# Halving the PSUM pools at the seams of a two-layer diffusion backbone, and modulation vectors first in the work paced beside attention

## The chip, the cores and the metric

The kernel runs on one core of a Trainium2 chip. The metric is the device time of one execution in microseconds; given is the median of three runs.

## What is computed

Two transformer layers over 512 latent tokens with 256 context tokens ahead of or beside them, width 1024, float32. Layer 0 mixes tokens by windowed grouped-query attention (16 heads of 64, 4 key heads, a sink logit, a window of 128 latent neighbours plus all context keys), layer 1 by a bidirectional gated linear recurrence (HGRN2). Each layer ends in a gated channel mixer with a 3-tap convolution. Every part is normalised and modulated first:

```python
def layer(x, ctx, mixer):
    h = rms_norm(x) * (1 + scale) + shift      # shift, scale, gate = SiLU(c) @ ada_w
    x = x + gate * mixer(h)                    # attention, or HGRN2
    h = rms_norm(x) * (1 + scale2) + shift2
    u, g = split(h @ w_up)                     # 2816 wide each
    x = x + gate2 * ((conv3(u) -> silu) * g) @ w_down
    return x
...
s = concat([q @ k_window, q @ k_ctx, sink])    # one softmax, sink column dropped
```

Latent and context rows are modulated by vectors of their own. The output is the latent stream.

## The kernel before, in words

Products are float32 split into a high and a low part (wh, wl for weights), so each needs three matmuls. A tile framework schedules the program: the order in which the program is written gives each instruction its priority, a simulated timeline orders each engine's queue, and tiles come from pools. PSUM has eight banks of 512 float32 columns. A pool opened where an older pool was closed lies over the same banks, and its first tile waits for the last users of those banks. So which pool lies where sets what a stage's first matmul waits for. Weights come in raw through two buffers of 1 MB (`wp`, tile `wr`; the modulation weights `wada` use the same two), SyncE issues the loads in program order, ACT copies a high part (L117, L140) and DVE makes the low part (L118, L141).

The stages, with their places in the profiled execution:

- First norm and the key and value projections, to about 97 us. Its last pools are psP0 (banks 0 to 2), psP1 (3 to 5) and psTA (6 and 7).
- Attention, 97 to 358 us (`attention`). 4 key groups times 6 query tiles are 24 units. `attend` computes scores S for four heads of a unit (L785, L786), their maximum nm on DVE (L809), exponentials on ACT (L795), and normalises on POOL (L797); query tiles of the context have tiles Sc and Pc. `weigh`, one unit later, transposes the weights of the softmax (pt, L829), copies them out (L832, L834) and multiplies with V (pv, L837, copied out as o in L839). `q_proj` projects a query group (pjq, L611). PSUM: psS 2 buffers of 2 banks (0 to 3), psT (4, 5), psV (6), psP (7).
- Beside attention runs paced work, the generator `others` (L851 to L860): after each unit, steps are taken until they have cost `PER_UNIT`. Its items are the query projections of groups 1 to 3 and two sets of modulation vectors (`ada_steps`, L301: eight k-steps, each one load of 1 MB and four matmuls `ada`, and a last step that transposes the result, `adat`).
- Output projection, 342 to 424 us (`attn_out`, product ao, transposes xT of the input x; `add_gated` evicts on DVE, L908). ao's pool pj lies in banks 0 to 3, that of xT, ppA, in 4 to 7.
- First channel mixer, 424 to 977 us: up products in sums and differences of halves (tiles pZ, pY, pV, L188, from part sums hs that DVE makes, L384), statistics nss and nR, down products dn (L170) evicted by DVE (L1024, tiles xl, xc). All tiles come from one pool of eight banks in turn.
- HGRN, 977 to about 1425 us (its first product is pf, from the normalised hn), with the pools sc (0, 1), pj (2 to 5) and lv (6, 7); its output product ho, to 1453.
- Second channel mixer, 1454 to 1821 us, for latent rows alone, again from one pool of eight banks; row factors from the sum of squares acc (nss, L536).

Of the kernel before, what the change touches and what calls it, by code (L numbers as in the profile page):

```python
# [14 lines left out]
PSUM = bass.MemoryType.PSUM  # L15
# [57 lines left out]
class Kernel:  # L73
    def __init__(self, tc, a, dbg=None):
        self.tc, self.nc, self.a, self.dbg = tc, tc.nc, a, dbg or {}
# [576 lines left out]
    def attention(self, hn):  # L652
        nc, a, tc = self.nc, self.a, self.tc
        win = a["attn_w_in"][0]
        es = ExitStack()
# [90 lines left out]
        with e1:  # L746
            tmp = self.ap_ = self.pool(e1, "atmpA", 2)
            self.ap_tag = "qraw"
            psP = kv["pool"]
            psT = self.pool(e1, "psTA", 2, PSUM)  # L750
# [7 lines left out]
        qp.append(self.pool(es, "qp1", 1))  # L758
        pb = self.pool(es, "pb", 3)
        sm = self.pool(es, "sm", 3)  # L760
        psS = self.pool(es, "psS", 2, PSUM)
        psT = self.pool(es, "psT", 2, PSUM)
        psV = self.pool(es, "psV", 1, PSUM)
        psP = self.pool(es, "psP", 1, PSUM)
        ORD = (0, 2, 1, 3)

        def attend(g, qt):
# [26 lines left out]
            def finish(j, sp, p, n):  # L794
                nc.scalar.activation(p[:, :n + 1], sp, AF.Exp, bias=nm[:, j:j + 1], accum_out=den[:, j:j + 1])  # L795
                nc.vector.reciprocal(r[:, j:j + 1], den[:, j:j + 1])
                nc.gpsimd.tensor_scalar(p[:, :n], p[:, :n], r[:, j:j + 1], 1.0, op0=ALU.mult, op1=ALU.mult)  # L797
                pr.append(p)

            if lat:  # L800
                masks = ([(lo, 128)] if qt > 0 else []) + ([(LAT - P, 256)] if qt < NQ - 1 else [])
                for j, h in enumerate(ORD):
                    if j % 2 == 0:
                        p = pb.tile([P, 2, 644], F32, tag="P", name="P", bufs=4)
                    sp = psS.tile([P, 1024], F32, tag="S", name="S")
                    scores(sp, lo, h, kb0 * P, (kb1 + 1) * P, masks)
                    scores(sp, LAT, h, LAT, TOK, [])
                    sink_col(sp, TOK, h)
                    nc.vector.tensor_reduce(nm[:, j:j + 1], sp[:, lo:TOK + 1], axis=AX.X, op=ALU.max, negate=True)  # L809
                    finish(j, sp[:, lo:TOK + 1], p[:, j % 2], nk)  # L810
            else:
                for j0 in (0, 2):
                    p = pb.tile([P, 2, 644], F32, tag="P", name="Pc", bufs=4)
                    sp = psS.tile([P, 2, 512], F32, tag="S", name="Sc")
                    for j in range(2):
                        scores(sp[:, j], 0, ORD[j0 + j], LAT, TOK, [])
                        sink_col(sp[:, j], CTX, ORD[j0 + j])
                    nc.vector.tensor_reduce(nm[:, j0:j0 + 2], sp[:, :, :CTX + 1], axis=AX.X, op=ALU.max, negate=True)
                    for j in range(2):
                        finish(j0 + j, sp[:, j, :CTX + 1], p[:, j], CTX)  # L820
# [30 lines left out]
        def others():  # L851
            def ada(l, r):
                for _ in self.ada_steps(l, r, psP, "pj", 512):
                    yield 0.9

            yield from q_proj(psP, psT, 1)
            yield from ada(0, 1)
            for g in (2, 3):
                yield from q_proj(psP, psT, g)
            yield from ada(0, 2)  # L860

        work = others()
# [92 lines left out]
    def ffn(self, l, hs, R, rows, lat_only, tmp, acp, bk, gp, done, side=None):  # L955
        nc, a = self.nc, self.a
# [41 lines left out]
        for r, nf in enumerate(ROUNDS[l]):  # L998


            coming = list(range(f0 + nf, f0 + nf + (*ROUNDS[l], 0)[r + 1]))
            ahead = []
            for dp in range(KT // 2):
                if len(ahead) < len(coming) and (lat_only or dp == 0):
                    ahead.append(up(coming[len(ahead)]))
                if side and r < 5 and dp == 0:
                    next(side, None)
                w = self.load_w([wdn[f0 * P:(f0 + nf) * P, dp * 256:dp * 256 + 256].rearrange("(k p) m -> p k m", p=P)], True)
                outs = [[(bank("dn")[:, 0:m], c) for _, c, m in segs] for _ in range(2)]

                def down(j, ks):
# [308 lines left out]
    def run(self, stop=99):  # L1320
        nc, a = self.nc, self.a
# [17 lines left out]
        self.wsp.append(wsC)  # L1339
        Rp = self.pool(top, "Rp", 1)  # L1340
        pjs = ExitStack()
        pj = self.pool(pjs, "pj", 2, PSUM)
        hB = ExitStack()
        hb = self.pool(hB, "hB")
        h1 = hb.tile([P, 4, 2, 4, 386], F32R, tag="hn", name="hs0")
# [3 lines left out]
        es = ExitStack()  # L1349
# [3 lines left out]
        hs = [*(h1[:, i] for i in range(4)), h2]  # L1353
        with ExitStack() as e2:
            pp = self.pool(e2, "ppA", 2, PSUM)
            xsp = self.pool(e2, "xsp", 2)
            self.attn_out(oh, hs, acc, _Multi(tmp, xsp, ("xs",)), pj, pp)
        pjs.close()
        rs.close()
        if stop == 2:  # L1360
            self.dump_x(); es.close(); hss.close(); hB.close(); top.close(); return
        bk = self.pool(pjs, "bkA", 8, PSUM)
        h3 = self.pool(rs, "hs2", right=True).tile([P, 2, 2, 4, 386], F32R, tag="hs", name="hs5")
        hs += [h3[:, i] for i in range(2)]
        gp = self.pool(es, "gpA", 5)
# [24 lines left out]
        es = ExitStack()  # L1390
# [2 lines left out]
        self.wsp = [self.ws0, wsC, self.ws0, wsD]  # L1393
        e2 = ExitStack()
        sc = self.pool(e2, "sc", 2, PSUM)
        pj = self.pool(e2, "pj", 2, PSUM)
        lv = self.pool(e2, "lv", 2, PSUM)
        part = self.hgrn(hn2[0], R, accs[0], hb, pj, lv, sc)
        hc = self.pool(rs, "hC", 1, right=True)
        hs1 = hc.tile([P, 7, 2, 4, 258], F32R, tag="hs", name="hs3")  # L1400
# [15 lines left out]
        gp = self.pool(es, "gpB", 9)  # L1416
        self.wsp = [self.ws0, wsC, self.ws0, wsD, self.pool(es, "wsE", 2)]
        self.wd = self.pool(es, "wd", 2)
        bk = self.pool(es, "bkB", 8, PSUM)
        rows = self.row_factor(acc, True, tmp, bk, "ps", 512, R, -1.0, (gp, "g"))  # L1420
        ost = {}

# [21 lines left out]
class _Halves:  # L1444
# [5 lines left out]
    def tile(self, *a, **kw):  # L1450
        return self.parts.pop(0)


class _Multi:


# [28 lines left out]
```

## Time and profile before

| | |
|---|---|
| median of 3 runs | 1826.52 us (1824.79 to 1827.17) |
| profiled execution | 1823.13 us, its span 1821.1 us |
| mean granted TensorE clock | 0.995 of full |
| TensorE matmul busy | 97% of the span |
| TensorE weight loads | 85% |
| DVE, ACT, POOL | 73%, 46%, 14% |
| HBM read | 162 MB, 90 GB/s |

Every instruction runs on its engine's queue in order. A timeline row gives start, busy time, engine, line, operation, output from inputs, and, in brackets, how long the engine stood idle before it and what released it. Rows of the same kind are joined with their count. The columns of the table of stretches are the length, busy time and instructions of TensorE's matmuls, its weight loads, DVE, ACT and POOL, then the granted clock, the share of DMA time and the rate.

### The profile page before, as it was taken

What the parts mean: (1) busy time and instruction counts of PE and PEld (TensorE: products, weight loads), DVE (VectorE), ACT (ScalarE), POOL (GpSimd) and SP (SyncE); (2) the same over time, 40 slices, a digit from 0 to 9 for tenths busy, and PEclk for the clock granted to TensorE, in tenths of its full rate; (3) what the DMA queues carried; (4) which work ended last, traced back from release to release, by engine and by line L of the source; (5) the groups of instructions that cost most, each with busy time, mean ns of one, the idle gap of its engine ahead of it and who ended that gap; (6) DMA issues with size and microseconds to landing.
All of it is one profiled execution on the core that took longest, in us unless ns stands there. A gap on an engine that the chain in (4) does not pass through costs nothing.

```text
span 1821.1 us, 32329 instructions
## 1 busy us (share of the span) xinstructions
PE 1762.3 (97%) x13062; PEld 1542.3 (85%) x13062; DVE 1327.0 (73%) x2420; ACT 840.9 (46%) x1754; POOL 253.2 (14%) x233
## 2 busy tenths in 40 slices
PE   6999999998999999999999999999999989999998
PEld 4986786687889888999998888889886789999997
DVE  6575576467777775867877667777776789998985
ACT  4344555465534452534455333333332556555553
POOL 1233233200101010101100101111110012011110
PEclk9999999999999999999999999999999989999999
DMA  9203203332333343221214221111225234333222
GB/s 310 76 24 140 70 24 139 85 106 88 110 110 107 114 139 93 93 70 58 71 44 122 59 59 39 56 48 47 59 71 185 71 93 118 107 112 105 84 69 81
DMA packets 204611, 166.44 MB, mean 91 GB/s; under 512 B 5341, under 2 KB 198446, under 8 KB 199342
## 3 DMA queue, kind: packets, MB, share of 16 engines
q1 hardware_dynamic: 196800, 160.47, 28.8%
q10 hardware_dynamic: 7662, 3.92, 0.7%
q8 instruction: 102, 1.67, 0.4%
q14 instruction: 47, 0.39, 0.1%
HBM read 162.27 MB, written 2.10 MB: 90 GB/s over the span
## 4 chain that ended last, share of the span: by engine, by line
PE 87%; DVE 5%; DMA 4%; ACT 2%; issue 1%; SPq 0%; POOL 0%; ACTq 0%; DVEq 0%; POOLq 0%
PE dn L170 16%; PE pZ L188 15%; PE pf L170 8%; PE pV L188 7%; PE pjq L611 4%; PE pv L170 4%; PE pY L188 4%; PE ao L170 4%; PE pgate L170 3%; PE pq L170 3%; PE pv L837 3%; PE pt L829 2%; PE ho L170 2%; PE kv L611 2%; PE ada L309 2%; DMA wr<-in_ffn_w_up 2%
## 5 line engine op out<-in xcount | busy, mean ns | idle before, releaser
L188 PE MATMUL pZ<-hs,wh 128*128 128x386 f32 (+1 forms) x1408 | 315.9, 314 | 4.7 <-DVE xl L908 1.5
L140 ACT ACTIVATE wh<-wr 128x512 fp32r<-128x512 f32 x264 | 163.3, 629 | 236.2 <-PE pZ L188 85.5
L170 PE MATMUL dn<-g,wh 128*128 128x512 f32 (+1 forms) x1056 | 266.0, 357 | 0.1
L188 PEld LDWEIGHTS pZ<-hs,wh 128*128 128x128 f32 x1408 | 240.9, 191 | 18.4 <-issue 7.8
L117 ACT ACTIVATE wh<-wr 128x512 fp32r<-128x512 f32 (+2 forms) x192 | 113.4, 601 | 280.8 <-PE pf L170 75.7
L141 DVE TENSOR_TENSOR wl<-wr,wh 128x512 fp32r<-128x512 f32 x264 | 190.8, 732 | 47.3 <-ACT wh L140 42.9
L188 PE MATMUL pZ<-hs,wl 128*128 128x386 f32 (+1 forms) x704 | 218.1, 313 | 3.2 <-DVE wl L141 3.2
L170 PEld LDWEIGHTS dn<-g,wh 128*128 128x128 f32 x1056 | 172.8, 188 | 26.1 <-ACT wh L117 0.4
L923 POOL TENSOR_TENSOR gg<-gg,R 128x772 f32<-128x772 f32 (+1 forms) x44 | 92.5, 2101 | 727.1 <-DVE gg L922 637.9
L118 DVE TENSOR_TENSOR wl<-wr,wh 128x512 fp32r<-128x512 f32 (+2 forms) x192 | 132.2, 698 | 70.3 <-ACT wh L117 58.2
L188 PE MATMUL pV<-hs,wh 128*128 128x386 f32 (+1 forms) x704 | 160.7, 314 | 2.4 <-DVE hs L384 1.8
L170 PE MATMUL dn<-g,wl 128*128 128x512 f32 (+1 forms) x528 | 158.9, 356 | 0.0
L188 PEld LDWEIGHTS pZ<-hs,wl 128*128 128x128 f32 x704 | 133.3, 190 | 6.7 <-DVE wl L141 4.8
L188 PEld LDWEIGHTS pV<-hs,wh 128*128 128x128 f32 x704 | 120.9, 191 | 5.2 <-DVE hs L384 2.8
L170 PE MATMUL pf<-hn,wh 128*128 128x512 f32 (+1 forms) x512 | 117.6, 344 | 2.5 <-DVE xc L1024 1.9
L188 PE MATMUL pV<-hs,wl 128*128 128x386 f32 (+1 forms) x352 | 110.5, 314 | 0.3 <-DVE wl L141 0.3
L170 PEld LDWEIGHTS dn<-g,wl 128*128 128x128 f32 x528 | 87.5, 188 | 14.2
L1024 DVE SCALAR_TENSOR_TENSOR xl<-dn,mod,xl 128x512 f32<-128x512 f32 x96 | 71.3, 747 | 37.2 <-PE dn L170 37.0
L170 PEld LDWEIGHTS pf<-hn,wh 128*128 128x128 f32 x512 | 79.2, 189 | 15.0 <-DVE xc L1024 2.2
L188 PE MATMUL pY<-hs,wh 128*128 128x386 f32 (+1 forms) x352 | 80.3, 313 | 4.6 <-ACT wh L140 4.3
L611 PE MATMUL pjq<-wh,hn 128*128 128x256 f32 x384 | 77.8, 290 | 0.0
L188 PEld LDWEIGHTS pY<-hs,wh 128*128 128x128 f32 x352 | 59.3, 189 | 10.5 <-ACT wh L140 8.7
(301 smaller groups left out, 3853.4 us busy)
## 6 DMA issues: line engine op xcount, KB each, us to landing
wr<-in_ffn_w_up SPq DMA_DIRECT2D x88, 512.0 KB, 5.0
wada<-in_ada_w SPq DMA_DIRECT2D x40, 1024.0 KB, 4.8
wr<-in_hgrn_w_in SPq DMA_DIRECT2D x40, 512.0 KB, 4.0
wd<-in_ffn_w_down SPq DMA_DIRECT2D x20, 512.0 KB, 4.0
ar<-in_ada_w SPq DMA_DIRECT2D x32, 256.0 KB, 7.0
wr<-in_attn_w_in SPq DMA_DIRECT2D x6, 1024.0 KB, 8.4
wr<-in_ffn_w_down SPq DMA_DIRECT2D x12, 384.0 KB, 3.2
wr<-in_attn_w_out SPq DMA_DIRECT2D x8, 512.0 KB, 5.1
```

The source lines that it names most:

```text
L117: nc.scalar.activation(wh, src, AF.Copy)
L118: nc.vector.tensor_tensor(wl, src, f(wh), op=ALU.subtract)
L140: nc.scalar.activation(ops[i][0], src, AF.Copy)
L141: nc.vector.tensor_tensor(ops[i][1], src, f(ops[i][0]), op=ALU.subtract)
L170: nc.tensor.matmul(o, lhsT=wt, rhs=at[:, t0:t0 + o.shape[1]], start=(first and n == 0 and i == 0), stop=(last and n == len(ks) - 1 and i = ...
L188: self.nc.tensor.matmul(ps, lhsT=wt, rhs=at, start=(first and k == 0 and i == 0), stop=(k == nk - 1 and i == 2), skip_group_check=not first)
L309: nc.tensor.matmul(ps[32 * j:32 * j + 32, 0:512], lhsT=self.cs[:, k, :], rhs=raw[:, j * 512:(j + 1) * 512], start=(k == 0), stop=(k == KT ...
L611: nc.tensor.matmul(out, lhsT=x, rhs=y[:, wk], start=(start and k == 0 and j == 0), stop=(stop and k == KT - 1 and j == 2))
L829: nc.tensor.transpose(pt[:, j * P:(j + 1) * P], pr[j][:, b * P:(b + 1) * P], self.ident)
L837: nc.tensor.matmul(pv[a * HD:(a + 1) * HD, 0:256], lhsT=V[:, tl, g, :], rhs=pT[:, a * 256:(a + 1) * 256], start=(b == 0), stop=(b == len(t ...
L923: times = lambda eng, o, x, y: eng.tensor_tensor(o, x, y, op=ALU.mult)
L1024: nc.vector.scalar_tensor_tensor(x[:, d], o, self.modc(l, v, 5, d), x[:, d], op0=ALU.mult, op1=ALU.add)
```

## The change

Every stage's PSUM pools are cut into smaller ones or change places, so that tiles lie over other banks. `_Turn` hands out tiles from its pools by turns, after those in `first`. In attention S tiles alternate between psS0 (banks 0, 1) and psS1 (3, 4), pt between psT0 (2) and psT1 (6), with psP in 5 and psV in 7. In the output projection ppA now lies in banks 0 to 3 and pj in 4 to 7. Both channel mixers have two pools of four banks; in the last round of the first, the last two steps take all their four banks from one of them each. In HGRN lv changes places with pj. The paced work starts with the first set of modulation vectors, and three of its steps are taken unpaid inside the very first unit, after head j=1. No instruction is added or removed.

```diff
-        psS = self.pool(es, "psS", 2, PSUM)
-        psT = self.pool(es, "psT", 2, PSUM)
+        psS0 = self.pool(es, "psS0", 1, PSUM)
+        psT0 = self.pool(es, "psT0", 1, PSUM)
+        psS = _Turn([psS0, self.pool(es, "psS1", 1, PSUM)])
+        psP = self.pool(es, "psP", 1, PSUM)
+        psT = _Turn([psT0, self.pool(es, "psT1", 1, PSUM)])
         psV = self.pool(es, "psV", 1, PSUM)
-        psP = self.pool(es, "psP", 1, PSUM)
...
                     finish(j, sp[:, lo:TOK + 1], p[:, j % 2], nk)
+                    if g == 0 and qt == 0 and j == 1:
+                        for _ in range(3):
+                            next(work)
...
-            yield from q_proj(psP, psT, 1)
             yield from ada(0, 1)
-            for g in (2, 3):
+            for g in (1, 2, 3):
                 yield from q_proj(psP, psT, g)
             yield from ada(0, 2)
...
                 w = self.load_w([wdn[f0 * P:(f0 + nf) * P, dp * 256:dp * 256 + 256].rearrange("(k p) m -> p k m", p=P)], True)
+                if not lat_only and not coming and dp >= 2:
+                    bk.first = [bk.home[1 - dp % 2]] * 4
...
-        pj = self.pool(pjs, "pj", 2, PSUM)
...
             pp = self.pool(e2, "ppA", 2, PSUM)
+            pj = self.pool(e2, "pj", 2, PSUM)
...
-        pjs.close()
...
-        bk = self.pool(pjs, "bkA", 8, PSUM)
+        bk = _Turn([self.pool(pjs, "bkA0", 4, PSUM), self.pool(pjs, "bkA1", 4, PSUM)])
...
         sc = self.pool(e2, "sc", 2, PSUM)
+        lv = self.pool(e2, "lv", 2, PSUM)
         pj = self.pool(e2, "pj", 2, PSUM)
-        lv = self.pool(e2, "lv", 2, PSUM)
...
-        bk = self.pool(es, "bkB", 8, PSUM)
+        bk = [self.pool(es, "bkB0", 4, PSUM), self.pool(es, "bkB1", 4, PSUM)]
+        bk = _Turn(bk, bk[:1] * 3)
...
+class _Turn:
+    def __init__(self, pools, first=()):
+        self.home, self.pools, self.first = pools, pools, list(first)
+
+    def tile(self, *a, **kw):
+        if self.first:
+            return self.first.pop(0).tile(*a, **kw)
+        self.pools = self.pools[1:] + self.pools[:1]
+        return self.pools[-1].tile(*a, **kw)
```

Three places of TensorE's queue, before and in the change. An entry in brackets names what an instruction waits for; PE_ there stands for TensorE's own earlier work, DMAHW for loads. Lines are those of the kernel concerned, and L788 of the change is L785 of before.

The start of attention, from the end of head j=0's or j=1's scores to the third head's. Before:

```order
L788 LDWEIGHTS cbf
L788 MATMUL S<-cbf 128x128
L785 MATMUL S<-KA,qT_1104 128x256
L786 MATMUL S<-KB,qT_1104 128x256
L792 LDWEIGHTS one_385
L792 MATMUL S<-sinkp,one_385 128x1
L785 MATMUL S<-KA,qT_1104 128x256 [waits Activation_49]
L786 MATMUL S<-KB,qT_1104 128x256
L788 LDWEIGHTS cbf
L788 MATMUL S<-cbf 128x128
L785 MATMUL S<-KA,qT_1104 128x256
```

In the change:

```order
L788 MATMUL S<-KA,qT_1104 128x256
L789 MATMUL S<-KB,qT_1104 128x256
L795 LDWEIGHTS one_385
L795 MATMUL S<-sinkp,one_385 128x1
L309 MATMUL ada<-wada,cs 32x512 [waits DMAHW1_49]
L309 MATMUL ada<-wada,cs 32x512 x3
L309 MATMUL ada<-wada,cs 32x512 [waits DMAHW2_49]
L309 MATMUL ada<-wada,cs 32x512 x3
L788 MATMUL S<-KA,qT_1104 128x256 [waits Activation_49]
L789 MATMUL S<-KB,qT_1104 128x256
```

Two modulation steps of four matmuls each, on the first two loads, now stand between the second and the third head.

The end of attention, from the last unit's transposes on. Before:

```order
L829 MATMUL pt<-cst,Pc 128x128 [waits PE_49]
L829 MATMUL pt<-cst,Pc 128x128 x3
L829 MATMUL pt<-cst,Pc 128x128 [waits Pool_49]
L170 MATMUL ao<-oh,wh 128x512 [waits Activation_49]
L170 MATMUL ao<-oh,wh 128x256
L170 MATMUL ao<-oh,wh 128x512
L170 MATMUL ao<-oh,wh 128x256
L170 MATMUL ao<-oh,wl 128x512
```

In the change:

```order
L836 MATMUL pt<-cst,Pc 128x128 [waits Pool_49]
L836 MATMUL pt<-cst,Pc 128x128
L844 MATMUL pv<-pT,V 64x256 [waits DVE_49,Activation_49]
L844 MATMUL pv<-pT,V 64x256
L844 MATMUL pv<-pT,V 64x256 [waits Activation_49]
L844 MATMUL pv<-pT,V 64x256
L902 MATMUL xT<-cst,xs 128x128 [waits DMAHW0_49,PE_49]
...
L170 MATMUL ao<-oh,wh 128x512 [waits Activation_49]
L170 MATMUL ao<-oh,wh 128x256
L170 MATMUL ao<-oh,wh 128x512
```

The output products ao, which stood between the last transposes and the last products with V, stand behind these and behind the transposes xT.

The first channel mixer's last down products and HGRN's first product. Before:

```order
L170 MATMUL dn<-g,wh 128x256
L170 MATMUL dn<-g,wl 128x512 [waits DVE_49]
L170 MATMUL dn<-g,wl 128x256
L170 MATMUL pf<-hn_9837,wh 128x512 [waits DVE_49]
L170 MATMUL pf<-hn_9837,wh 128x258
```

In the change:

```order
L170 MATMUL dn<-g,wh 128x256
L170 MATMUL dn<-g,wl 128x512 [waits DVE_49]
L170 MATMUL dn<-g,wl 128x256
L170 MATMUL pf<-hn_9848,wh 128x512 [waits PE_49]
L170 MATMUL pf<-hn_9848,wh 128x258
```

The order is the same; pf waits for TensorE's own earlier work in place of DVE's.

On SyncE the load of the second query group's weights moves behind the eight loads `wada` of the first set of modulation vectors, and its four splits on ACT and DVE move behind that set's last step.

## Rows read from the trace of the kernel before

**Rows 1.** The page, part 1: busy time, share and instructions of each engine.

```profile
PE 1762.3 (97%) x13062; PEld 1542.3 (85%) x13062; DVE 1327.0 (73%) x2420; ACT 840.9 (46%) x1754; POOL 253.2 (14%) x233
```

**Rows 2.** Stretches: length, busy time by engine, granted clock, DMA share, GB/s.

```profile
120.00:200.00 80.00, 79.81 (x624) 56.72 (x623) 49.00 (x114) 39.49 (x98) 25.25 (x32) 1.00 0.35 119
200.00:320.00 120.00, 120.00 (x935) 89.01 (x934) 80.98 (x190) 67.16 (x164) 41.69 (x52) 1.00 0.17 62
```

**Rows 3.** Waits of TensorE: total us, times, longest us.

```profile
PE nss L536 <- DVE acc L527: 2.3, 1, 2.3
```

**Rows 4.** Timeline of TensorE at attention's start: start, us, instruction, idle before.

```profile
101.51 0.39 PE L785 MATMUL S<-KA,qT 128*128 128x256 f32 x1 [0.77 <-ACT qraw L616]
...
102.23 0.18 PE L792 MATMUL S<-sinkp,one 96*128 96x1 bf16 x1
...
106.14 0.38 PE L785 MATMUL S<-KA,qT 128*128 128x256 f32 x1 [3.01 <-ACT P L795]
...
112.29 0.45 PE L785 MATMUL S<-KA,qT 128*128 128x384 f32 x1 [0.43 <-ACT P L795]
```

**Rows 5.** Timelines of DVE and ACT, same place.

```profile
99.78 0.69 DVE L118 TENSOR_TENSOR wl<-wr,wh 128x512 fp32r<-128x512 f32 x1
...
104.60 0.68 DVE L809 TENSOR_REDUCE nm<-S 128x1 f32<-128x513 f32 x1
...
105.31 0.69 ACT L795 ACTIVATE P<-S,nm 128x513 f32<-128x513 f32 x1 [0.78 <-DVE nm L809]
```

**Rows 6.** Stretches behind two holes, columns as in rows 2.

```profile
106.40:109.90 3.50, 3.50 (x21) 3.17 (x20) 2.78 (x10) 1.94 (x5) 3.13 (x3) 0.54 0.39 166
1461.00:1472.00 11.00, 9.74 (x40) 8.06 (x38) 10.18 (x21) 5.84 (x13) 2.33 (x1) 0.54 0.30 99
```

**Rows 7.** Timeline of TensorE: modulation steps; last, landing of their loads.

```profile
158.48 1.92 PE L309 MATMUL ada<-wada,cs 128*32 128x512 f32 x16
...
DMA to landing us min/median/max: 4.8/4.9/4.9
```

**Rows 8.** Stretch of attention's end without paced work, columns as in rows 2.

```profile
325.60:346.30 20.70, 19.42 (x146) 13.01 (x144) 13.00 (x33) 12.44 (x38) 6.19 (x11) 1.00 0.23 63
```

**Rows 9.** Attention to output projection: ao alone in one stretch; timelines of TensorE, POOL, ACT.

```profile
346.20:358.00 11.80, 9.05 (x48) 7.35 (x48) 0.00 (x0) 1.00 0.00 0
...
351.04 0.98 PE L829 MATMUL pt<-cst,Pc 128*128 128x128 f32 x7
...
355.69 1.08 PE L837 MATMUL pv<-pT,V 128*64 128x256 f32 x8
...
357.98 1.47 PE L896 MATMUL xT<-cst,xs 128*128 128x128 f32 x12
361.01 1.66 PE L170 MATMUL ao<-oh,wh 128*128 128x512 f32 x8 [1.56 <-ACT wh L117]
...
345.50 1.84 POOL L797 TENSOR_SCALAR Pc<-Pc,r 128x256 f32<-128x256 f32 x4 [4.12 <-DVE r L796]
...
352.06 0.60 ACT L832 ACTIVATE pT<-pt 128x512 f32<-128x512 f32 x1 [0.52 <-PE pt L829]
356.82 0.38 ACT L839 ACTIVATE o<-pv 128x256 f32<-128x256 f32 x1 [4.16 <-PE pv L837]
```

**Rows 10.** Timeline of TensorE behind the output projection.

```profile
425.60 1.07 PE L309 MATMUL ada<-wada,cs 128*32 128x512 f32 x8 [1.47 <-DVE y L422]
```

**Rows 11.** Timelines of TensorE and DVE, first channel mixer to HGRN.

```profile
976.52 0.52 PE L170 MATMUL dn<-g,wl 128*128 128x512 f32 x2
978.94 0.98 PE L170 MATMUL pf<-hn,wh 128*128 128x512 f32 x4 [1.90 <-DVE xc L1024]
...
978.40 0.48 DVE L1024 SCALAR_TENSOR_TENSOR xc<-dn,mod,xc 128x256 f32<-128x256 f32 x1
...
982.53 0.48 DVE L363 SCALAR_TENSOR_TENSOR hn<-xc,gs,hn 128x256 fp32r<-128x256 f32 x1
```

**Rows 12.** Timeline of TensorE, HGRN to the second channel mixer.

```profile
1454.34 0.48 PE L188 MATMUL pZ<-hs,wh 128*128 128x258 f32 x2 [1.54 <-DVE xl L908]
```

## The prediction

> **What bounds the kernel now.** I read the page first, then the stretches stage by stage, then the waits of TensorE, and last the timelines around the places that the change touches. TensorE is busy 97% of the span [rows 1], so time can only come out of its holes, some 59 us, and out of stretches at the lower clock. The stretches say where holes are not: between 120 and 320 us it is busy 199.8 of 200 us [rows 2]. Work that the change reorders inside that stretch pays nothing and costs nothing as long as TensorE stays full; work pulled out of it into a hole is paid back in full, because the stretch becomes that much shorter. The holes lie at the seams between stages. The list of waits names them, as nss for acc [rows 3], and each timeline gives its place: S for the exponentials, ada for y, pf for xc, pZ for xl [rows 4, 10 to 12].
>
> All my terms are against the profiled execution (1823.13 us, span 1821.1). It stands 3.4 us under the median of 1826.52; I add the sum to the median.
>
> **1. Attention start.** The first S waits 0.77 us for qraw, an evacuation from an older pool, and the third S (head j=2) waits 3.01 us for the first exponential [rows 4]. The chain of that wait stands in the queues of DVE and ACT [rows 5]: S of j=0 was written at 102.41 [rows 4], but its maximum nm only starts at 104.60, behind the splits wl of the second query group's weights, and the exponential starts at 105.31. The change does three things here. (a) The first S lies over banks that the older stage leaves sooner; TensorE no longer waits for qraw. (b) That group's weight load goes behind eight loads of modulation weights, so four wl splits leave this piece of DVE's queue, 0.69 us each (one of them at 99.78) and some 2.4 in all, as ends overlap. Two steps stq now stand ahead of nm and take back about 1. I expect the third S at about 104.9, 1.2 us sooner. (c) Two of the three unpaid modulation steps stand between the second and the third S. A step is four matmuls, eight records; two steps take 1.92 us [rows 7]; the idle that can take them is what is left of 3.01, so all of 1.9 goes in, but the exponential is then waited for only if it is later than that. The third step stands before the later waits, where 0.43 is idle [rows 4]. The steps' weights: the first load takes the place in the queue of the query load, long before, the second that of the first load, so both are there.
> The second head takes 0.72 like the first, to 103.13; both end 0.77 sooner, near 102.4, and with 1.9 behind them TensorE is free at 104.3, before 104.9: both fit, and nothing is counted twice. So 1.2 + 1.9 + 0.4: -3.5 without the clock. Bounds: -1.4 if the third S starts no sooner than 106.14 and one of the two steps finds its weights late (0.96 + 0.43), -4.2 if all idle of this place (0.77 + 3.01 + 0.43) goes.
>
> [...]
>
> **2. Loads behind the modulation steps.** Before, the eight steps ran in a full stretch, and a load of 1 MB needed 4.9 us to land [rows 7]. Now they run in the first two attention units with the order fixed. Two buffers alternate, so a step's load can only be issued when the step two places ahead is done. Between step 4 and step 6 (counted from 0) stand about 4.8 us of TensorE work against a step's own end, the issue and 4.9 to land, some 5.6: 0.8 us of wait. Between step 6 and the first projection of the next query group stands some 8.5 us of work against a load and a split of about 6.7, which holds. I take +0.8, from 0 to +2; while these wait, scores queued behind them wait too, and so do the exponentials of ACT.
>
> **3. The end of attention without filler.** The three unpaid steps and the new order let the paced work run out earlier. From 325.6, where the last modulation vector was done, to 346.3 TensorE did 19.42 of 20.70 us [rows 8]: 1.28 us idle in 11 of the head-wise score groups. In the order of the change 20 groups are left when the last modulation vector is done, so some 17 us more run this way: 1.28 x 17 / 20.7 = +1.0, between 0 and +2.
>
> **4. Attention to output projection.** Now the first product ao fills the wait between the last weighings: between 346.2 and 358 it does 9.05 us of work in pieces, and xT follows [rows 9]. In the change ao's pool lies over the banks of the last score, transpose and value tiles, so the order puts all of ao behind the last pv and behind xT. This cover is gone; what is late next? The last weighing's chain without ao in between: POOL normalises Pc at 345.50 for 1.84, then the transposes (0.98), a copy (0.60) and pv (1.08), with handovers that I put at 0.4 in all: pv ends near 350.4. xT's 1.47 follows, over the copy of o (0.38), so ao starts near 351.9 and is through at 351.9 + 9.05 = 361.0. Before, TensorE reached the same point at 357.98 + 1.47 and stood until 361.01 for wh, an idle of 1.56 that now is filled. So 0. Bounds: -0.4 without the handovers, and +6.3 if the last pv still ended at 356.77 and xT and all of ao came behind it (367.3 against 361.01).
>
> **5. Output projection to the first channel mixer.** ada waits 1.47 us for DVE's y [rows 10], a bank that is held. In the change this wait is gone, but the part sums that DVE makes (hs) are the later bound of the next 15 us, and DVE's order hardly moves. I take -0.5, from 0 to -2.5.
>
> **6. First channel mixer to HGRN.** The last dn ends at 976.52 + 0.52 = 977.04; pf starts at 978.94, after 1.90 us, when DVE's xc has released the last banks at 978.88 [rows 11]. The change gives the last two steps of the last round all four banks of one half each, and HGRN's first product the half that ends sooner. pf then waits only for TensorE. That the last two steps take one half each is costed at nothing: two of a half's four banks were left a step before, and the other two are evicted while the first two fill. Next is the input: the last hn of this sub-layer is written at 983.0, while pf comes to its eighth k only after seven of 0.98 us or more, at 983.9. So -1.9 whole; the bounds are -1.0 (hn later by one eviction of 0.75 to 0.9) and -1.9.
>
> **7. HGRN to the second channel mixer.** pZ waits 1.54 for DVE's xl [rows 12] and nss 2.3 for acc [rows 3], and the clock is 0.54 over the 11 us from 1461 [rows 6], up to 5.0 us of TensorE time. The change lets the first pZ run between the output products, so the 1.54 is filled. But acc comes from DVE, after the last output product's eviction; that product ends later for what was put between, and nss waits as before. DVE is busy 10.18 of those 11 us, so a better clock is worth little while DVE makes the inputs. I take -0.8, from +1.5 (output products pushed back by the whole 1.54) to -5.
>
> No instruction is added or removed. The orders of HGRN's middle are unchanged and count nothing.
>
> Sum: -3.5 - 0.4 + 0.8 + 1.0 + 0 - 0.5 - 1.9 - 0.8 = -5.3. As a check, the holes that go (0.77, 3.01, 0.43, 1.90, 1.54, 1.47 = 9.1) exceed that. 1826.5 - 5.3 = **1821.2 us**.
>
> **The rivals.**
> *A. The holes move.* TensorE fills a hole and then waits for the same exponential, the same acc, the same hs, since these are made by ACT and DVE. For it: DVE is busy in nearly all of 1461 to 1472 [rows 6]. Against it: at pf and at the first nm the queue is what is late, not the data. Terms: -1.4 + 0.8 + 1.0 + 0 + 0 - 1.0 + 0 = -0.6: 1825.9. That the banks were not what these places wait for, so that the change doesn't do what it says, comes out here as well.
> [...]
> *C. Attention's end runs dry.* ao has lost its cover. It decides if the last pv ends later than about 350.4: each microsecond adds one, and from 353 on TensorE has had little to do for several microseconds, so its clock would fall as it did after 1460. With the full +6.3, 5.0 lost at the low level as there, and term 3 at +2: -5.3 + 6.3 + 5.0 + 1.0 = +7.0, 1833.5, slower. The sum leaves the banks of no change (3.7) once ao is late by 9 us, clock included. For it: the loss of cover is certain; against it: ACT stands idle 4.16 us before its last copy of o [rows 9], so nothing holds the chain but ao in TensorE's queue. [...]
>
> **How the numbers follow.** Forecast 0.52, A 0.23, B 0.12, C 0.13. About 0.2%, 3.7 us, is what a measurement of this kernel can tell from no change. The forecast's own range is 1817 to 1825, two thirds of it beyond 3.7: 0.34 faster, 0.18 same; B is faster (0.12); A is nearly all same (0.02 faster, 0.21 same); C is slower 0.11, same 0.02. In all: faster 0.48, same 0.41, slower 0.11. The range leaves out half of C and a little of B: 1815.0 to 1829.0.
>
> **What would show it.** Right: two modulation steps behind the second S, the third S under 105.3; no wait of pf on xc; the first ao within 6.5 us of the last normalisation's start on POOL; nss still waiting 1.5 or more. Wrong: waits of ada on its weights over 2 us before 140; a granted clock under 0.9 between 346 and 362; dn waiting for xl or xc in the last two steps of its last round.

## The result, and the profile after

The changed kernel takes 1810.05 us, median of 4 runs (1808.85 to 1814.26), against 1826.85 us of the kernel before in 4 runs (1824.79 to 1829.05). The ratio is 0.991, 95% interval 0.9893 to 0.9927: 0.9% faster, some 16 us, three times what was forecast and outside the range. The profiled execution took 1809.72 us with a span of 1807.9 us, 13.2 us less than the span before.

Where the 13 us lie is seen by laying the same marks in both timelines of TensorE (us between the starts of the first matmul named, or the end of the last one):

| stretch | before | after | difference |
|---|---|---|---|
| start to the first S | 101.51 | 100.66 | -0.85 |
| first S to the end of the last ao | 322.62 | 316.18 | -6.44 |
| to the first dn | 76.57 | 74.60 | -1.97 |
| first dn to the first pf | 478.24 | 470.94 | -7.30 |
| pf to the first ho (HGRN) | 405.49 | 406.87 | +1.38 |
| first to last ho | 68.37 | 71.47 | +3.10 |
| to the end of TensorE's last matmul | 363.76 | 362.13 | -1.63 |

Two stretches make nearly all of it, attention and the first channel mixer; what lies behind gives a little back. The mean granted clock of the whole execution did not rise: 0.993 after, 0.995 before.

The page's line of busy times of the kernel after, which answers to [rows 1]:

```profile
PE 1760.6 (97%) x13062; PEld 1543.7 (85%) x13062; DVE 1324.9 (73%) x2420; ACT 840.5 (46%) x1754; POOL 248.7 (14%) x233
```

TensorE's busy time is 1.7 us less at the same count of instructions; the rest of the 13.2 us is time in which it stood idle before and no longer does. The waits of TensorE after (total us, times, longest), which answer to [rows 3]:

```profile
PE pY L188 <- ACT hs L383: 3.4, 1, 3.4
...
PE nss L536 <- DVE acc L527: 1.7, 1, 1.7
...
PE S L788 <- ACT P L798: 1.5, 3, 0.7
PE pq L170 <- DVE z L1086: 1.5, 1, 1.5
```

S waits 1.5 us in all and no longer 4.4; pf's wait for xc, 1.9 before, is gone; a wait of pq for z and one of pY for hs are new.

**Attention's start.** TensorE's timeline after, which answers to [rows 4]:

```profile
100.66 0.36 PE L788 MATMUL S<-KA,qT 128*128 128x256 f32 x1
...
102.18 1.92 PE L309 MATMUL ada<-wada,cs 128*32 128x512 f32 x16
104.03 0.38 PE L788 MATMUL S<-KA,qT 128*128 128x256 f32 x1
...
106.77 0.44 PE L788 MATMUL S<-KA,qT 128*128 128x384 f32 x1 [0.30 <-ACT P L798]
...
108.36 1.06 PE L309 MATMUL ada<-wada,cs 128*32 128x512 f32 x8 [0.55 <-DMA wada<-in_ada_w]
```

The first S waits for nothing. The two modulation steps follow the second head at 102.18, and the third S starts at 104.03, straight behind them: it does not wait at all, where it had waited 3.01 us. In DVE's queue the first maximum nm starts at 102.08 (104.60 before) and the two steps stq stand behind it, so the first exponential, from 102.80 to 103.49, is done before the modulation steps are. Left of this place's idle are 0.30 and the 0.55 that the third step waits for its weights. The stretch from 100 to 125 us, before and then after (columns as in [rows 2]):

```profile
100.00:125.00 25.00, 20.79 (x158) 18.05 (x157) 18.16 (x43) 13.22 (x30) 8.20 (x9) 0.93 0.12 43
```

```profile
100.00:125.00 25.00, 24.15 (x195) 14.73 (x194) 17.98 (x42) 13.36 (x31) 10.28 (x11) 1.00 0.73 259
```

Before, TensorE was busy for 20.79 us at 0.93 of its clock; counted at the full clock that is by an estimate 1.75 less (25 x 0.07), 19.0. After, it is 24.15 at 1.00. The difference, 5.1 us of TensorE's work at full clock, is what this place gave: 3.4 of it were idle and 1.75 went to the low clock. The estimate takes TensorE's time to grow as the clock falls; in the trace before, the same three products of S (KA, KB, cbf) take 0.36 us from start to start at 102.27, at a clock of 1.00, and 0.66 at 107.79, at 0.50. The split is bookkeeping; the experiments show that part of a longer low stretch is hidden behind other waits (0.86 in place of 0.93 over these 25 us cost at most 0.4).

**Attention's end.** Timelines of POOL and TensorE after, which answer to [rows 9]:

```profile
338.97 1.85 POOL L800 TENSOR_SCALAR Pc<-Pc,r 128x256 f32<-128x256 f32 x4 [4.57 <-DVE r L799]
...
342.98 1.08 PE L844 MATMUL pv<-pT,V 128*64 128x256 f32 x8 [0.77 <-ACT pT L839]
344.00 1.53 PE L902 MATMUL xT<-cst,xs 128*128 128x128 f32 x12
345.28 0.95 PE L170 MATMUL ao<-oh,wh 128*128 128x512 f32 x4
```

From the last normalisation's start to ao it takes 6.31 us. ao then runs without a hole.

**The first channel mixer.** The waits of TensorE inside it, in the kernel before (480 to 976 us) and after (472 to 962 us):

```profile
PE pZ L188 <- DVE wl L141: 2.4, 2, 1.3
PE pY L188 <- ACT wh L140: 2.1, 4, 0.6
PE pZ L188 <- ACT wh L140: 0.4, 1, 0.4
```

```profile
PE pZ L188 <- DVE wl L141: 0.2, 1, 0.2
PE dn L170 <- ACT g L998: 0.2, 1, 0.2
```

The waits for weight splits, 4.9 us in seven places, shrink to 0.2. One of these places, at 729.06 in the kernel before: TensorE's row, and DVE's queue ahead of the split that it waits for:

```profile
729.06 0.45 PE L188 MATMUL pZ<-hs,wl 128*128 128x386 f32 x1 [1.12 <-DVE wl L141]
...
727.26 0.56 DVE L923 TENSOR_TENSOR G<-pZ,R 128x386 f32<-128x386 f32 x1
727.73 0.68 DVE L136 TENSOR_TENSOR wr<-wr 128x512 f32<-128x512 f32 x1
728.32 0.68 DVE L141 TENSOR_TENSOR wl<-wr,wh 128x512 fp32r<-128x512 f32 x1
```

The split wl at 728.32 stands behind the eviction G from pZ and a sum for the next weights. DVE's queue after, at the same place of the program:

```profile
714.53 0.56 DVE L929 TENSOR_TENSOR G<-pZ,R 128x386 f32<-128x386 f32 x1 [1.04 <-PE pZ L188]
715.52 1.29 DVE L141 TENSOR_TENSOR wl<-wr,wh 128x512 fp32r<-128x512 f32 x2 [0.43 <-ACT wh L140]
716.93 0.69 DVE L136 TENSOR_TENSOR s<-wr 128x512 f32<-128x512 f32 x1
717.54 1.02 DVE L991 SCALAR_TENSOR_TENSOR u<-G,par,u 128x770 f32<-128x770 f32 x1
```

Two splits now stand directly behind G, and the sums (s) and u behind them. When pZ comes to its wl at 718.58, the split has been done for almost 2 us. TensorE's own queue differs here too. Before, the two products with wh (727.42) are followed at once by the one with wl that waits; after, products pY stand between them:

```profile
716.46 0.52 PE L188 MATMUL pZ<-hs,wh 128*128 128x386 f32 x2
...
718.58 0.34 PE L188 MATMUL pZ<-hs,wl 128*128 128x386 f32 x1
```

Even without these pY, the split, which ends at 716.81, would have come in time for a wl straight behind the two products.

**HGRN.** TensorE's timeline after, 21 us behind the first pf:

```profile
983.60 0.75 PE L170 MATMUL pq<-hn,wh 128*128 128x256 f32 x4 [1.53 <-DVE z L1086]
```

pq waits 1.53 us for z, which DVE makes. There was no such wait before: most of what pf gained at its start is given back here.

**Entry to the second channel mixer.** TensorE's timeline and the stretch around it after, which answer to [rows 12] and [rows 6]:

```profile
1445.17 0.58 PE L188 MATMUL pY<-hs,wh 128*128 128x258 f32 x1 [3.37 <-ACT hs L383]
1447.50 1.87 PE L536 MATMUL nss<-cst,acc 128*128 128x2 f32 x8 [1.75 <-DVE acc L527]
...
1445.00:1475.00 30.00, 26.88 (x181) 25.54 (x182) 26.41 (x50) 15.64 (x33) 4.30 (x2) 0.83 0.38 105
```

The hole of 1.54 us ahead of pZ is gone, but pY waits 3.37 for hs and nss still waits 1.75, and the granted clock of these 30 us is 0.83, the same as in the 30 us from 1454.30 before.

### The profile page after: what moved, and what is told of

It reads as the page before. It is cut to its first block, busy times and chain, and to the rows that moved or that the text cites. A ratio compares the mean times of both kernels' runs of the same rounds, so it can differ in the third digit from the quotient of the medians.

```text
span 1807.9 us, 32327 instructions
## 1 busy us (share of the span) xinstructions
PE 1760.6 (97%) x13062; PEld 1543.7 (85%) x13062; DVE 1324.9 (73%) x2420; ACT 840.5 (46%) x1754; POOL 248.7 (14%) x233
## 4 chain that ended last, share of the span: by engine, by line
PE 87%; DMA 5%; DVE 5%; ACT 2%; issue 1%; SPq 0%; ACTq 0%; DVEq 0%
PE dn L170 16%; PE pZ L188 15%; PE pf L170 8%; PE pV L188 7%; PE pjq L611 4%; PE pv L170 4%; PE ao L170 4%; PE pY L188 3%; PE pgate L170 3%; PE pq L170 3%; PE pv L844 2%; PE ho L170 2%; PE pt L836 2%; PE kv L611 2%; DMA wr<-in_ffn_w_up 2%; PE ada L309 2%
## 5 line engine op out<-in xcount | busy, mean ns | idle before, releaser
L929 POOL TENSOR_TENSOR gg<-gg,R 128x772 f32<-128x772 f32 (+1 forms) x44 | 87.4, 1986 | 722.8 <-DVE gg L928 657.8
L188 PEld LDWEIGHTS pV<-hs,wl 128*128 128x128 f32 x352 | 67.1, 191 | 4.5 <-DVE wl L141 1.8
```

What stands on the lines that cost most here:

```text
L188: self.nc.tensor.matmul(ps, lhsT=wt, rhs=at, start=(first and k == 0 and i == 0), stop=(k == nk - 1 and i == 2), skip_group_check=not first)
L929: times = lambda eng, o, x, y: eng.tensor_tensor(o, x, y, op=ALU.mult)
```

## The experiments

Two theories after the result. **A**: the gain is a sum of places, each won by the edit made there: attention by its pools and its order of work, the first channel mixer by its two halves. **B**: the waits inside the first channel mixer go because everything in front ends elsewhere in time, a shift. All ratios are to runs of the kernel before on the same chip, with 95% intervals.

**Attention alone.** Edit: the pools of `attention`, `others` and the three unpaid steps as in the change, all else as before.

> Only the attention part: its pools, the modulation steps first, the three unpaid steps; all else as before. Theory A (the change's gain is the sum of its places, each won where its own pools are): the last output product of attn_out ends 5 to 8 us sooner than before, everything behind keeps its length, so 5 to 8 us in all. Theory B (the gain inside the first channel mixer is a shift that comes from starting elsewhere in time, not from its own banks): 10 us or more, with the waits of pZ and pY for weight splits between 480 and 905 us (some 5 us in all before) mostly gone here too.

Ratio 0.9954 (0.9936 to 0.9972), some 8 us. From the first S to the last ao 316.77 us (322.62 before, 316.18 in the change). The first dn to pf takes 477.67: the inside of the mixer is as slow as before. Theory B is out.

**The output projection's pools alone.**

```diff
-        pj = self.pool(pjs, "pj", 2, PSUM)
...
             pp = self.pool(e2, "ppA", 2, PSUM)
+            pj = self.pool(e2, "pj", 2, PSUM)
...
-        pjs.close()
```

> Only the output projection's two pools change places (ao behind the last weighing). By the prediction's term 4, about 0 here (-0.4 to +6.3), plus up to -2.5 at the entry to the first channel mixer. Theory A: 0 to -3, and nothing changes inside the first channel mixer or behind it. Theory B: a shift alone changes the waits for weight splits there by several us either way.

Ratio 1.0017 (0.9998 to 1.0035), no gain. From the first S to the last ao 322.60 us, before 322.62: losing ao as a filler costs nothing, as the chain of the prediction's term 4 had it. TensorE's timeline there:

```profile
352.98 1.08 PE L837 MATMUL pv<-pT,V 128*64 128x256 f32 x8 [0.77 <-ACT pT L832]
354.54 0.97 PE L170 MATMUL ao<-oh,wh 128*128 128x512 f32 x4 [0.47 <-ACT o L839]
```

ao waits 0.47 for the copy of o and follows the last pv. From the last ao to pf 557.2 us, within what the kernels with the old eight-bank pool show (554.8 to 558.0).

**The first channel mixer's banks alone.**

```diff
-        bk = self.pool(pjs, "bkA", 8, PSUM)
+        bk = _Turn([self.pool(pjs, "bkA0", 4, PSUM), self.pool(pjs, "bkA1", 4, PSUM)])
...
+                if not lat_only and not coming and dp >= 2:
+                    bk.first = [bk.home[1 - dp % 2]] * 4
```

> Only the first channel mixer's banks: two pools of four by turns, and one half for each of the last two down steps. Theory A: the wait of pf for xc (1.9) goes and with it some 5 us of waits for weight splits between 480 and 905 us, so -6 to -8. Theory B: only pf's 1.9 goes, -1 to -3, and the waits inside stay.

Ratio 0.9971 (0.9955 to 0.9987), some 5 us. From the first dn to pf 470.62 us, as in the change (470.94). One part of the expectation failed, as pf still waits:

```profile
976.80 0.97 PE L170 MATMUL pf<-hn,wh 128*128 128x512 f32 x4 [1.12 <-DVE xc L1026]
```

1.12 us, since its pool still lies where it lay before.

**The late pools alone.** Edit: HGRN's lv ahead of pj, and two pools in the second channel mixer.

> Only HGRN's pool order and the second channel mixer's two pools. Both theories: the change's trace is 15.2 us ahead at the end of HGRN's pf products and 13.7 at the end, so this part alone is no gain: -1 to +3 us, with the first pZ between the output products ho, and these ending up to 3 us later.

Ratio 1.0019 (1.0 to 1.0038): no gain. The first pZ stands 12.8 us ahead of the last ho's end, as expected. In this profile the ho stretch took 78.8 us, 10.4 more than before. Of that, 2.7 are waits of TensorE for the modulation weights (4.7 in this stretch, 2.0 before), and more than half is busy time, at a granted clock of 0.94 against 1.00. These waits in the whole execution:

```profile
PE ada L309 <- DMA wada<-in_ada_w: 6.5, 4, 3.5
```

In the kernels before and after this is 2.2 and 2.3. Over all profiles it goes from 1.9 to 6.6, with no relation to the edits that these runs show.

**Attention split in two.** First its pools alone, then the order of the work alone:

> Attention's pools of the change alone, with the work beside it in the old order. Theory A (the pools give the first S its 0.77 us, the order of the work gives the rest): the hole of 3.01 us ahead of the third S and the low clock behind it stay; the last output product of attn_out ends 0 to 2 us sooner than before, counted from the first S. Theory B (the pools let S run two banks ahead and keep TensorE fed): 4 us sooner or more, without the reordered work.

> The reordered work alone (modulation steps first, three of them unpaid), on the old pools. Theory A: the third S comes at 104 to 105 us, the granted clock behind it is 1.00, and attn_out ends 3.5 to 6 us sooner, counted from the first S. Theory B: the old pools make S wait for POOL's or ACT's release whatever stands between, so less than 2 us.

Ratios 0.9985 (0.9965 to 1.0005) and 0.9987 (0.9967 to 1.0007); from the first S to the last ao 320.33 and 319.09 us. Neither time alone can be told from no change; what follows is read from the traces. With the pools alone neither theory came out: the hole went against A, and the 2.3 us against the profile before are less than B's 4. With the order alone theory A's numbers came out (third S at 104.37, clock 1.00, 3.5 us). So each half alone takes the 3.01 us hole away, but not by the same means. TensorE's timeline with the pools alone:

```profile
102.19 0.36 PE L611 MATMUL pjq<-wh,hn 128*128 128x256 f32 x1
...
107.73 0.28 PE L787 MATMUL S<-KA,qT 128*128 128x256 f32 x1
```

The first projection of the next query group fills the hole, from 102.19 to the third S at 107.73. That it can run there because its pool now lies in another bank is read from the layout of the pools and was not tested apart. With the order alone:

```profile
101.29 0.39 PE L785 MATMUL S<-KA,qT 128*128 128x256 f32 x1 [0.25 <-ACT qraw L616]
...
103.89 0.66 PE L691 MATMUL qkT<-cst,stq 128*128 128x128 f32 x4 [0.98 <-DVE stq L724]
104.37 0.39 PE L785 MATMUL S<-KA,qT 128*128 128x256 f32 x1
...
114.38 1.92 PE L309 MATMUL ada<-wada,cs 128*32 128x512 f32 x16
```

The third S comes at 104.37 on the old pools, 3.08 us after the first, where it was 4.63 before and 3.37 in the change. The unpaid modulation steps have no part in it: on the old pools the first of them runs at 114.38. What went is the wait itself: without the four splits in DVE's queue the first maximum starts at 102.82 and the exponential at 103.54 (104.60 and 105.31 before).

The stretch from 100 to 125 us with the pools alone, with the order alone, and in the run that changed the mixer alone, where the hole stayed:

```profile
100.00:125.00 25.00, 23.43 (x191) 20.10 (x191) 20.72 (x53) 13.85 (x32) 9.77 (x11) 1.00 0.13 43
```

```profile
100.00:125.00 25.00, 23.20 (x186) 16.35 (x186) 19.24 (x47) 16.09 (x37) 11.14 (x12) 1.00 0.29 104
```

```profile
100.00:125.00 25.00, 21.22 (x157) 18.68 (x156) 18.70 (x44) 13.70 (x31) 7.74 (x9) 0.86 0.12 43
```

With the hole filled the clock is 1.00, in all six profiles of such kernels. With the hole it is 0.93 in three profiles and 0.86 in five. The lower value does not cost twice as much. With the mixer alone, one of the five, the clock falls while TensorE still stands idle in the hole (0.84 from 103.0 to 106.1, 1.00 before), and the wait of 0.43 that follows the hole in the three [rows 4] is gone in the five. From the first S to the first product with V it takes 20.3 us in the three and 20.3 to 20.7 in the five: at most 0.4 more. The gains of the halves overlap at this hole; what the two add beyond it was not told apart.

**A bank of its own for the modulation steps.** In the kernel before, the tile that the steps fill is held through many turns of the eight banks.

```diff
-        bk = self.pool(pjs, "bkA", 8, PSUM)
+        bk = self.pool(pjs, "bkA", 7, PSUM)
+        bkS = self.pool(pjs, "bkS", 1, PSUM)
```

> The kernel before with one edit: the modulation steps of the first channel mixer get a bank of their own and the other tiles seven banks by turns; the order inside that stage hardly moves against before, which it does in the change. Theory A (what frees the stage inside is the order of ACT's and DVE's queues that comes with two pools of four): the waits for weight splits stay, 478 us from the first dn to pf as before. Theory B (a modulation bank held over many turns stalls the rotation of eight): they go, 471 to 474 us.

Ratio 1.0018 (1.0 to 1.0036), first dn to pf 477.70 us. The waits inside (484 to 980 us) are those of before:

```profile
PE pZ L188 <- DVE wl L141: 2.6, 2, 1.4
PE pY L188 <- ACT wh L140: 2.0, 4, 0.6
...
PE pZ L188 <- ACT wh L140: 0.4, 1, 0.4
```

The held bank is not the cause; and at the place of the row at 729.06, DVE's queue still has G and the sum wr ahead of the split.

**Two halves by turns without the special last steps.** Edit: the first two lines of the mixer's diff above.

> Two pools of four by turns in the first channel mixer, without the halves for the last two down steps. Theory A (the queues' order inside comes from the turns): the waits inside stay away as in the run with both, and pf waits 1.9 for xc as before where that run showed 1.12: from the first dn to pf about 471.5 us. Theory B (the halves at the end matter for the inside): 476 us or more.

Ratio 0.9962 (0.9946 to 0.9978), first dn to pf 471.07 us, pf waits 1.90. The inside (484 to 972 us):

```profile
PE dn L170 <- ACT g L992: 0.3, 1, 0.3
PE pZ L188 <- DVE wl L141: 0.2, 1, 0.2
```

So the turns alone clear the inside, and the special steps alone move pf's wait from 1.90 to 1.12.

**Four pools of two.** Edit: `_Turn([self.pool(pjs, f"bkA{i}", 2, PSUM) for i in range(4)])`.

> The kernel before with the first channel mixer's eight banks in four pools of two by turns; the order inside that stage then differs both from before and from the change. Theory A (two halves free each bank in time): the waits for weight splits inside come back in part, 473 to 478 us from the first dn to pf. Theory B (what counts is only that DVE's and ACT's queues put the splits ahead of the evictions, and any order may do it or not): no number is excluded, 468 to 480, and where the waits go or stay the splits stand ahead or behind in the queues.

Ratio 0.9977 (0.9957 to 0.9997). From the first dn to pf 475.69 us, but that dn stands earlier among the products here; from the last ao to pf it is 552.86, before 554.81, with two halves by turns 548.38. The inside (488 to 976 us):

```profile
PE ada L309 <- DMA wada<-in_ada_w: 1.5, 1, 1.5
PE pZ L188 <- ACT wh L140: 0.6, 3, 0.2
PE pZ L188 <- DVE wl L141: 0.4, 2, 0.2
```

The number lies where theory A of this run had it, but the waits do not: of 4.9 us for splits 1.0 are left, the 1.5 is a load, and at the place of the row at 729.06 the two splits stand directly behind G, as they do in the change and with two halves by turns. Another division of the banks clears most of the inside too: halves are not special. TensorE's queue at this place, however, is that of before, with no pY between the products with wh and the one with wl:

```profile
734.71 0.45 PE L188 MATMUL pZ<-hs,wl 128*128 128x386 f32 x1 [0.19 <-DVE wl L141]
```

So here the splits' place in DVE's queue takes the wait from 1.12 to 0.19 without that change in TensorE's. Why the stretch from the last ao to pf is still 4.5 us longer than with two halves stays open; it is not idle, which is 8.2 us in both, but busy time, at a mean granted clock of 0.99 against 1.00. Besides, pf, with HGRN's pools as before, does not wait here either, and the time comes back at the same later place as in the change:

```profile
1001.67 0.74 PE L170 MATMUL pq<-hn,wh 128*128 128x256 f32 x4 [1.53 <-DVE z L1077]
```

From pf to the first ho this took 406.89 us, as in the change (406.87), against 405.5 in each run in which pf had waited 1.12 or 1.90.

**Output projection and mixer together.**

> Output projection's pools and the first channel mixer's banks together, the rest as before. From the last output product to pf before takes 554.8 us (554.8 to 558.3 in the runs with that part unchanged), the change 545.5, the mixer's banks alone 549.3, the output pools alone 557.2. Theory A (the entry to the mixer gains only where both are made: its first bank then lies over the pool of the input transposes, which ends sooner): 545 to 547 us here. Theory B (the rest of the gain comes from attention's end): 549 to 551 us.

Ratio 0.9959 (0.9943 to 0.9976); from the last ao to pf 547.87 us, between the two expectations: some 1.5 us less than with the mixer's banks alone, 1.2 to 2.3 short of the three runs that also have attention's edits (545.54, 546.32, 546.68). With attention's 0.9954 the product is 0.9913: the change's 0.991. (The 558.3 of that expectation is of the run with a bank of its own for the modulation steps, which changed that part; without it the highest is 558.0.)

**The change without each of its late parts.**

> The whole change but for the second channel mixer's two pools. Theory A (products Z and Y put between the output products ho cost more than they fill: the change's ho stretch is 3.1 us longer than before's): this is 0 to 4 us faster than the change, near 1808 us, with the hole of 1.54 us ahead of pZ back. Theory B (the first products fill what would be idle): 2 to 4 us slower than the change.

> The whole change but for HGRN's pool order. Every run with that order takes 406.9 to 407.1 us from pf to the first output product of HGRN, every run without it 405.5. Theory A (the order gives pf about 1.1 us and takes 1.4 in HGRN): within 0.5 us of the change, pf's wait 1.1, 405.5 us behind it. Theory B (pf's gain is real and the 1.4 come from elsewhere): 1 us slower than the change or more.

Ratios 0.9916 (0.9887 to 0.9945) and 0.9906 (0.9871 to 0.9942), 1812.3 and 1812.81 us: neither can be told from the change. Without HGRN's order pf waits 1.12 and HGRN takes 405.50, so that the two sums differ by 0.25. Without the mixer's two pools the ho stretch is 1.0 shorter and what follows 2.8 longer; which of that run's theories holds can't be told at this width. In both runs the first pZ stands behind the last ho again and waits 1.54 there: it moves ahead only with both parts. The stretch of ho itself takes 68.4 to 74.0 us in the profiles in which pZ stands behind it, so the change's 71.5 says nothing about its cost. No version's median was below the change's.

## Why the prediction was wrong

The sign was right and the size was not: -5.3 against some -16. By its own steps, against the profiled executions:

- **What bounds the kernel** was right about TensorE, and wrong in one sentence, "The holes lie at the seams between stages." **This is the step that failed most.** The first channel mixer has 4.9 us of waits for weight splits in its inside, seven places of 0.4 to 1.25 us, and the change's two pools of four reorder the queues there. The prediction never asked whether they would; it priced that edit at its last two down steps only (term 6). From the first dn to pf 7.3 us went, and 1.9 of them are pf's wait: 5.4 that the sum had at 0 without a reason. What it said of attention's full middle held: after, TensorE is busy 188.9 of the 190 us from 120 to 310.
- **Term 1** had the right places: the queue of DVE, the steps in the hole, and the third S at 104.03 for 104.9 forecast. It put the two steps stq ahead of nm at a cost of about 1; they stand behind it. Its division into queue order and filler is not confirmed, since the order alone brings the third S as early without a modulation step in the hole. It was too small, -5.1 (with the 0.85 before the first S, and with the third step's wait of 0.55) for -3.9. The -0.4 for the clock in the sum was the author's estimate, and no run shows that term; what the traces show is the granted clock of the 25 us, 0.93 before and 1.00 after, which the bookkeeping puts at 1.75.
- **Term 2**: +0.8 forecast, 0.55 found, inside the 5.1.
- **Term 3**: +1.0 forecast. From 300 us to the start of the last normalisation TensorE's idle is 1.5 us after and 1.0 before: +0.5, within its bounds.
- **Term 4** was right: 6.4 us from POOL's start to ao forecast, 6.31 found; no cost, alone or in the change.
- The last normalisation of attention starts 6.5 us sooner (345.50, 338.97). Terms 1 to 3 account for 4.6 of that; 1.9 stay unassigned. They lie within what attention scatters with its old pools and order: 322.6 to 327.6 us in eight profiles.
- **Term 5**: -0.5 forecast, -2.0 found, within its bounds. From the last ao to the first dn it takes 74.4 to 75.8 us in the four profiles with both the output pools and the mixer's banks, and 76.6 to 81.3 in the ten others, so it needs both. The gain is idle, 7.5 us before and 3.25 after; part of it went into busy time, 69.05 us before and 71.34 after for the same 381 products, at a granted clock of 0.98 and 0.93. The stretch before and after:

```profile
424.13:500.70 76.57, 69.05 (x381) 61.24 (x381) 59.15 (x100) 42.02 (x83) 9.65 (x8) 0.98 0.34 107
```

```profile
416.84:491.43 74.59, 71.34 (x381) 64.00 (x381) 59.32 (x103) 42.53 (x84) 9.34 (x8) 0.93 0.35 110
```

- **Term 6**: the 1.90 at pf went as forecast, but 1.4 came back as pq's wait for z. The prediction looked for what is late next only as far as the eighth k of pf.
- **Term 7**: -0.8 forecast; +1.5 from the first ho to the end in the profiles, which is within their scatter, and no difference in the runs without either part. nss's wait stayed as the term had it; pY's wait for hs (3.37), which ACT makes, it did not name.
- **The rivals.** A fell: in attention and in the mixer the queue was late and not the data; in HGRN and at the second mixer A was right. B, by which the clock stays up where holes are filled, was right at attention's start (0.93 before, 1.00 after). It was wrong at the second mixer, where the clock stayed at 0.83, and at the entry to the first, where it fell from 0.98 to 0.93. C did not happen: ao started in time, at a granted clock of 1.00.

The medians differ by more (16.8) than the profiled executions (13.4): the execution profiled before stood 3.4 us under its median. Its stretches to the last ao (322.62) and from there to the first dn (76.57) are the shortest, or within 0.01 us of it, of all profiles with those parts unchanged, so the profile before flatters it there.

What stays open: why the scheduler puts the splits ahead when the banks are divided. That DVE's queue is what frees TensorE is read from the rows at 729.06 and 715.52 and fits the other kernels at that place (own bank: splits behind, waits stay; turns and four pools: splits ahead, waits go). With two halves TensorE's own order moved there as well, and what each of the two orders gives over the whole stage was not told apart: no run changed an order with the banks left as they were.

## What to carry to other kernels

Where a scheduler orders the queues, a change of pools can change the order everywhere in their stage: compare the queues over the whole stage with the list of small waits there, not at its edges alone. The hole of 3.01 us in TensorE's work was closed in two ways, each alone enough here: by work that has a bank to run in, or by taking out of the way what stands ahead of the awaited instruction in another engine's queue. Filling holes did not by itself keep the clock up here: it rose at one seam, from 0.93 to 1.00 at attention's start, and fell at another, from 0.98 to 0.93 at the entry to the first mixer. A wait removed at the head of a stage is only worth what the next chain of that stage leaves: pf's 1.90 us went, and 1.53 came back at pq.

## What the runs showed that was not expected

- The granted clock around one and the same 3.0 us hole took two values over 25 us, 0.93 and 0.86, from profile to profile of equal code, and the lower one made the work behind it at most 0.4 us later.
- Waits for the same modulation loads swing with equal code: 0.16 to 2.41 us near 165 us in the eight profiles with attention as before; over the whole execution it is 1.9 to 6.6 us among all profiles.
